# Root mean square of the SSD group by column quarters, and another order of output and pooling pieces

## The chip, the cores and the metric

The kernel runs on one core of a Trainium2 chip. The metric is the device time of one execution in microseconds (us), as the median of several executions. The engines are named as the profile names them: PE is TensorE (PEld its weight loads), DVE is VectorE, ACT is ScalarE, POOL is GpSimd and SP is SyncE, which here only issues DMAs.

## The reference, cut to what matters

One layer of a diffusion backbone: a normalised and modulated input goes through one input projection; part of it feeds a bidirectional state space scan (SSD), part of it feeds a pooling mixer; both outputs share one output projection, and an MLP follows. The change is in the last lines of the mixer:

```python
def mixer_out(y_scan, xs, z, u, d_skip, ssm_norm_w, pool_w, pool_scale, w_out, grid):
    b, l = xs.shape[:2]
    y = y_scan + d_skip.astype(jnp.float32)[:, None] * xs
    y = y.reshape(b, l, SSM_GROUPS, -1) * jax.nn.silu(z).reshape(b, l, SSM_GROUPS, -1)
    y = rmsnorm(y, ssm_norm_w.reshape(SSM_GROUPS, -1)).reshape(b, l, D_SSM)
    pm = pool_mixer(u, pool_w, pool_scale, grid)
    return jnp.concatenate([y, pm], axis=-1) @ w_out.astype(jnp.float32)
```

There are 1024 tokens (two blocks b of 512) and 1024 SSD channels in two groups g of 512. So the norm of `y` is over four quarters (b, g), each of 4 tiles of 128 channels by 512 tokens. Pooling has four windows, each with 256 channels and a 256x256 matrix; the output projection multiplies 1024 normalised SSD channels and 1024 pooled channels.

## The kernel before, in words

Channels stand on the 128 partitions and tokens along the free axis. A dense product keeps float accuracy with three matmuls per 128x128 tile: operands are split into a rounded high part and a remainder, and `mm3` (L165) issues high x high (L172), high x low (L174) and low x high (L175). Weights come in pieces of 128 output channels, loaded by SP (`load_raw`, L115), split by ACT (`whi`) and DVE (`wlo`) in `split_raw` (L122). The pool `wp` has two buffers of each, so two split pieces exist at a time. The list `order` (L130 to L140) fixes the order of the pieces, `next_piece` (L157) takes the next and splits one ahead.

After the scan the list `units` (L134) sets the stage that the change touches. A unit "u" i is the input projection of the i-th pooling tile (`box_input`, L910), after which `box_diff` (L926) takes the box means of an earlier tile on DVE and writes them to DRAM (`d_d`). A unit "o" i is the SSD half of the output projection for output tile i: `out_ssm` (L972), 48 matmuls for both blocks, evicted by ACT into `sg` and written to `o_d`. A unit "p" i is a pooling matrix: `pool_mm` (L982) loads the differences (`dr`, L986), splits them (`dh` on ACT, `dl` on DVE), multiplies (tile `pw`, 24 matmuls, 12 for each block), and evicts into `pm_hi` (ACT, L994) and `pm_lo` (DVE, L995). After each "p", two rows of a modulation matrix are loaded (`wa`, L786) and summed on DVE (L81). The second half of the output projection, `out_pool` (L1084), needs all `pm` and adds to what `out_ssm` wrote (`mix`, read back at L1067).

`y_norm` (L875) is a generator, advanced between units by `step` (L1012). It loads the four quarters (`yt`, L881), then does for each quarter in turn: four squares on ACT (`y_sq`), one round of four matmuls with 32 columns of ones (L202, `SumSq.round`), each into a quarter of the partitions of one PSUM bank, one copy of these partial sums to SBUF (`sq<-ry`), one matmul with the full matrix `c512` that adds the 128 partial rows (L213), and a reciprocal square root on ACT and DVE (logarithm, exponential, square and a correction step in two DVE instructions, L217 to L221). These are float matmuls, and each shows as two instructions in the trace. Then it scales and splits the quarter (`yn_hi`, `yn_lo`, L901 to L903). The fourth quarter's factor is in `rs_r` of the pool `ypool`; `esY.close()` (L1014) gives that pool's space to the next `box_diff` tiles.

The instructions are not run in the order of the text. The framework plans the order of each engine's queue before the run: among the instructions that its own reckoning of durations says are ready, the one that stands first in the program goes first. `after` (L90) adds an order without a wait: the first square stands after the last weight split issued so far, the first sum after the last matmul issued so far. Once planned, each queue is worked off in order.

Of the kernel before, what the change touches and what calls it, by code (L numbers as in the profile page):

```python
# [8 lines left out]
F32 = mybir.dt.float32  # L9
# [6 lines left out]
P = 128  # L16
KT = 8
T = 1024
TB = 512
# [24 lines left out]
def hybrid_block(ctx, tc, A):  # L44
# [23 lines left out]
    def dense_ps(name):  # L68
        return psd.tile([P, TB], F32, tag="d", name=name)

    def pair_ps(name):
        return psm.tile([P, 2, TB], F32, tag="m", name=name)
# [4 lines left out]
    def stt(out, in0, s, in1, op0, op1):  # L77
        return ve.scalar_tensor_tensor(out=out, in0=in0, scalar=s, in1=in1, op0=op0, op1=op1)
# [8 lines left out]
    def act(out, in_, f, bias=0.0, scale=1.0):  # L87
        return ac.activation(out=out, in_=in_, func=f, bias=bias, scale=scale)  # L88

    def after(ins, prev):  # L90
        tc.add_manual_dep(
            ins.ins, prev.ins.name,
            mybir.DependencyInfo(mybir.DependencyClass.NoSync, mybir.DependencyReason.DATA),
            reason="order")
        return ins
# [36 lines left out]
    for m in range(8):  # L132
        order += [W[PX + m], W[PZ + m]]
    units = [("u", 0), ("u", 1), ("u", 2), ("u", 3), ("u", 4), ("o", 0), ("u", 5), ("o", 1), ("u", 6), ("o", 2),  # L134
             ("u", 7), ("o", 3), ("o", 4), ("o", 5), ("p", 0), ("o", 6), ("p", 1), ("o", 7), ("p", 2), ("p", 3)]
    for kind, i in units:
        order.append({"u": W[PU + i], "o": A["w_out"][0, i], "p": ("pool", i)}[kind])
    for m in (0, 1, 2, 3, 4, 5, 6, 7, 2, 3, 4, 5, 6, 7):
        order.append(A["w_out"][1, m])
    order += [A["w_mlp1"][m] for m in (0, 4, 1, 5, 2, 6)] * 2  # L140
# [16 lines left out]
    def next_piece(ahead=1):  # L157
        i = used[0]
        used[0] += 1
        fetch(i + 1 + ahead)  # L160
        return loaded[i]
# [19 lines left out]

    class SumSq:
        def __init__(self, n, nk, name, pool):
            self.pair = pair_ps(name)
# [21 lines left out]
        def rstd(self, comb, r=None):  # L208
            n = self.n
            part = self.tmp()  # L210
            act(part, self.ps[:, :n], AF.Copy)
            tot = self.pair[:, 1]
            pe.matmul(tot[:, :n], M[comb], part, start=True, stop=True)  # L213
            q = self.tmp()
            if r is None:
                r = self.pool.tile([P, self.pool.width], F32, tag="rs_r", name="rs_r", bufs=1)[:, :n]
            act(q, tot[:, :n], AF.Ln, bias=eps)  # L217
            self.exp = act(r, q, AF.Exp, scale=-0.5)
            act(q, r, AF.Square)
            stt(q, tot[:, :n], EPS, q, ALU.add, ALU.mult)  # L220
            stt(r, q, -3.0, r, ALU.add, ALU.mult)  # L221
            return r

    def modulated(src, r, G, sh, hi, lo, pool):
# [125 lines left out]
    def step(g, n=1):  # L350
        for _ in range(n):
            next(g, None)
# [503 lines left out]
    def y_tile(i, name, dt=F32):  # L856
        return yq.tile([P, 4, TB], dt, tag=f"y{i}", name=name)
# [17 lines left out]
    def y_norm():  # L875
        yt = []
        for i, (b, g) in enumerate(BG):
            if i == 1:
                yield
            yt.append(y_tile(i, "yt"))  # L880
            sy.dma_start(yt[i], yg_d[4 * g : 4 * g + 4, :, b * TB : (b + 1) * TB].rearrange("k p t -> p k t"))  # L881
        yield
        r_t = y_tile(8, "y_rs")
        rs = []
        for i in range(4):
            ssq = SumSq(TB, 4, "ry", yp_)
            sq_t = y_tile(4 + i, "y_sq")
            for k in range(4):
                sq = ssq.add(yt[i][:, k], later=True, sq=sq_t[:, k])
                if i == 0 and k == 0:  # L890
                    after(sq, last_split[0])
            rnd = ssq.round()
            if i == 0:
                after(rnd, last_mm[0])
            rs.append(ssq.rstd("c512", r_t[:, i] if i < 3 else None))
            yield
        for i, (b, g) in enumerate(BG):
            hi = y_tile((4, 6, 0, 2)[i], "yn_hi", F32R)
            lo = y_tile((5, 7, 1, 8)[i], "yn_lo", F32R)
            for k in range(4):  # L900
                stt(yt[i][:, k], yt[i][:, k], V("ssm_w", 4 * g + k, 1), rs[i], ALU.mult, ALU.mult)  # L901
                act(hi[:, k], yt[i][:, k], AF.Copy)
                tt(lo[:, k], yt[i][:, k], hi[:, k].bitcast(F32), ALU.subtract)  # L903
            yn[b, g] = (hi, lo)
            yield
# [20 lines left out]
    def box_diff(gi, m, cu):  # L926
        wd = WINDOWS[gi]
        h2 = wd // 2
        lev = wd.bit_length() - 1
        nh = 1 if wd == 2 else 2  # L930
        ru_t = up.tile([P, (GR + WM - 1) * GW], F32, tag="ru", name="ru")
        ru = ru_t[:, : (GR + wd - 1) * GW].rearrange("p (a b) -> p a b", b=GW)
        gp.memset(ru[:, 0:h2, :], 0.0)
        if h2 > 1:
            gp.memset(ru[:, h2 + GR :, :], 0.0)
        nr = GR // nh
        for hf in range(nh):
            src, n = cu[:, hf * nr : (hf + 1) * nr, :], GW + wd - 1
            for l in range(lev):
                s_ = 1 << l  # L940
                n -= s_
                if l == lev - 1:
                    dst = ru[:, h2 + hf * nr : h2 + (hf + 1) * nr, :]
                else:
                    dst = box_tile("bc", l)[:, : nr * n].rearrange("p (a b) -> p a b", b=n)
                tt(dst, src[:, :, 0:n], src[:, :, s_ : s_ + n], ALU.add)
                src = dst
        for a, b in ((0, h2), (GW - h2 + 1, GW)):
            if a < b:
                sub = ru[:, h2 : h2 + GR, a:b]  # L950
                tt(sub, sub, edge[:, gi, GR + a : GR + b].unsqueeze(1).broadcast_to([P, GR, b - a]), ALU.mult)
        dv = up.tile([P, GR, GW], F32, tag="dv", name="dv")
        ncl = GW // nh
        for hf in range(nh):
            cs_ = slice(hf * ncl, (hf + 1) * ncl)
            src, n = ru[:, :, cs_], GR + wd - 1
            for l in range(lev):
                s_ = 1 << l
                n -= s_
                if l == lev - 1:  # L960
                    dst = dv[:, :, cs_]
                else:
                    dst = box_tile("br", l)[:, : n * ncl].rearrange("p (a b) -> p a b", b=ncl)
                tt(dst, src[:, 0:n, :], src[:, s_ : s_ + n, :], ALU.add)
                src = dst
        for a, b in ((0, h2), (GR - h2 + 1, GR)):
            if a < b:
                tt(dv[:, a:b], dv[:, a:b], edge[:, gi, a:b].unsqueeze(2).broadcast_to([P, b - a, GW]), ALU.mult)
        stt(dv, dv, 1.0 / (wd * wd), cu[:, :, h2 : h2 + GW], ALU.mult, ALU.subtract)
        sy.dma_start(d_d[m], dv.rearrange("p a b -> p (a b)"))  # L970

    def out_ssm(m):  # L972
        w = next_piece()
        for b in range(NB):
            ps = dense_ps("mixp")
            mm3(ps, w, yn[b, 0], kn=4, stop=False)
            mm3(ps, w, yn[b, 1], k0=4, kn=4, start=False)
            t = sg.tile([P, TB], F32, tag="sg", name="sg")
            act(t, ps, AF.Copy)
            sy.dma_start(o_d[b][:, m], t)  # L980
# [23 lines left out]
    for kind, i in units:  # L1004
        if kind == "u":
            gi = i // 2
            box.append((gi, i, box_input(gi, next_piece())))
            nu += 1
            if nu > 1:
                box_diff(*box.pop(0))  # L1010
            if nu in (2, 3, 4):
                step(yn_steps, (0, 0, 5, 2, 3)[nu])  # L1012
            if nu == 3:
                esY.close()  # L1014
                ux = new_pool(esU, "ux", 1)
        elif kind == "o":
            out_ssm(i)
            if box and nu == 8:
                box_diff(*box.pop(0))
        else:  # L1020
            if pm is None:
                esK.close()
                esU.close()
                pm = [(poolA.tile([P, KT, TB], F32R, tag="A", name=f"pm_hi{b}"),
                       poolA.tile([P, KT, TB], F32R, tag="A", name=f"pm_lo{b}")) for b in range(NB)]
                esD = ctx.enter_context(ExitStack())
                dp = new_pool(esD, "dp", 2, side="right")
                crow2 = dp.tile([P, 1024], F32, name="crow2", bufs=1)
                sy.dma_start(crow2, c_d.broadcast_to([P, 1024]))
            pool_mm(i)  # L1030
            for j in range(16 + 2 * i, 18 + 2 * i):
                ada_rest(j, dp.tile([P, 1024], F32, tag="wa2", name="wa2"), crow2)
# [594 lines left out]
```

## Time and profile before

| | |
|---|---|
| median of 3 runs | 1444.07 us (1443.58 to 1445.48) |
| profiled execution | 1443.95 us, its span 1442.2 us |
| PE busy | 1397.7 us, 97% of the span |
| DVE busy | 1034.1 us, 72% |
| ACT busy | 733.7 us, 51% |
| mean granted TensorE clock | 0.991 |
| `y_norm` sums on PE | 472.0 to 496.6 us |
| first `out_ssm` matmul on PE | 518.8 us |
| first and last `pw` matmul on PE | 617.1 and 669.1 us |

A stretch row gives the start and end in us, then the busy time of each engine with the number of instructions, then the granted clock (1.00 is the full 2.4 GHz), DMA share and GB/s. A timeline row gives start, busy time, engine, line, operation, output and inputs, shape and count, and in brackets the idle time before it with what ended it. An x2 in a row of L202 or L213 is one matmul in float. Matmuls are pipelined, so what one costs is read from the start of one to the start of the next.

### The profile page before, as it was taken

The numbers are of one execution on the slowest core, as the hardware profiler recorded it, in microseconds if no ns is written. First come the engines' busy times: TensorE is split into PE (matmuls) and PEld (weight loads), VectorE is DVE, ScalarE is ACT, GpSimd is POOL, SyncE is SP. The second block draws the span as 40 slices with busy tenths as digits, with TensorE's granted clock in tenths as the row PEclk, the third lists the DMA queues.
The fourth block names the chain that finished last, engine by engine and source line by source line (L and its number), as shares of the span: only waits on it lengthen the run. The fifth ranks groups of instructions, "written<-read, shape, count | busy, mean of one in ns | idle before, by whom it ended". The sixth has DMA issues, their size and how long they took to land. (4 is left out here: it accounts for less than half of the span.)

```text
span 1442.2 us, 18171 instructions
## 1 busy us (share of the span) xinstructions
PE 1397.7 (97%) x6760; PEld 1092.0 (76%) x6760; DVE 1034.1 (72%) x1606; ACT 733.7 (51%) x1150; POOL 49.3 (3%) x100
## 2 busy tenths in 40 slices
PE   6999899999999999999999999999999999999996
PEld 2667778888887588877866687888887888888875
DVE  2699589987776699663667776665668787878626
ACT  4776565555553732243246665555566562535344
POOL 0000100000000000000000000000001000000000
PEclk8999999999999999999999999999999999999998
DMA  9421644542223332479533444433467463645703
GB/s 386 163 66 55 135 135 136 151 108 78 79 75 97 134 103 102 147 258 379 193 117 110 139 170 173 158 135 134 149 215 258 143 209 96 186 136 168 249 21 117
DMA packets 77177, 218.60 MB, mean 152 GB/s; under 512 B 8993, under 2 KB 15265, under 8 KB 74658
## 3 DMA queue, kind: packets, MB, share of 16 engines
q1 hardware_dynamic: 67058, 186.25, 39.9%
q0 software_dynamic: 10032, 31.20, 5.9%
q8 instruction: 53, 0.87, 0.2%
q14 instruction: 34, 0.28, 0.1%
HBM read 164.07 MB, written 53.35 MB: 151 GB/s over the span
## 5 line engine op out<-in xcount | busy, mean ns | idle before, releaser
L172 PE MATMUL dn<-h_hi,whi 128*128 128x512 f32 x448 | 179.3, 400 | 1.1 <-ACT Cf L88 1.1
L174 PE MATMUL dn<-h_lo,whi 128*128 128x512 f32 x448 | 177.4, 396 | 0.0
L175 PE MATMUL dn<-h_hi,wlo 128*128 128x512 f32 x448 | 177.3, 397 | 0.0
L1242 PE MATMUL sx<-hop,wop 128*128 128x512 f32 x432 | 169.6, 392 | 1.4 <-ACT acc L88 1.4
L1243 PE MATMUL sx<-hop,wop 128*128 128x512 f32 x432 | 170.3, 394 | 0.0
L1244 PE MATMUL sx<-hop,wop 128*128 128x512 f32 x432 | 168.7, 391 | 0.0
L88 ACT ACTIVATE wop<-raw 128x512 fp32r<-128x512 f32 x162 | 101.1, 626 | 104.5 <-PE syw L1244 47.4
L85 DVE TENSOR_TENSOR wop<-raw,wop 128x512 fp32r<-128x512 f32 x162 | 111.4, 689 | 48.2 <-ACT wop L88 47.7
L88 ACT ACTIVATE whi<-raw 128x1024 fp32r<-128x1024 f32 (+1 forms) x76 | 78.6, 1034 | 129.5 <-PE mixp L174 52.1
L1242 PE MATMUL syw<-hop,wop 128*128 128x512 f32 x324 | 127.6, 394 | 2.8 <-DVE stage L85 2.8
L85 DVE TENSOR_TENSOR wlo<-raw,whi 128x1024 fp32r<-128x1024 f32 (+1 forms) x76 | 90.6, 1193 | 52.8 <-ACT whi L88 52.3
L1243 PE MATMUL syw<-hop,wop 128*128 128x512 f32 x324 | 128.1, 395 | 0.0
L1244 PE MATMUL syw<-hop,wop 128*128 128x512 f32 x324 | 127.0, 392 | 0.0
L172 PEld LDWEIGHTS dn<-h_hi,whi 128*128 128x128 f32 x448 | 84.2, 188 | 24.7 <-issue 7.4
L174 PEld LDWEIGHTS dn<-h_lo,whi 128*128 128x128 f32 x448 | 84.2, 188 | 22.1 <-issue 6.0
L175 PEld LDWEIGHTS dn<-h_hi,wlo 128*128 128x128 f32 x448 | 84.2, 188 | 20.4 <-issue 3.8
L88 ACT ACTIVATE hop<-hraw 128x512 fp32r<-128x512 f32 x116 | 70.9, 627 | 52.9 <-DMA hraw<-hid_d 52.3
L1242 PEld LDWEIGHTS sx<-hop,wop 128*128 128x128 f32 x432 | 81.2, 188 | 20.7 <-ACT acc L88 1.8
L1244 PEld LDWEIGHTS sx<-hop,wop 128*128 128x128 f32 x432 | 81.2, 188 | 18.2
L1243 PEld LDWEIGHTS sx<-hop,wop 128*128 128x128 f32 x432 | 81.2, 188 | 17.8
L85 DVE TENSOR_TENSOR hop<-hraw,hop 128x512 fp32r<-128x512 f32 x116 | 77.0, 687 | 13.0 <-ACT hop L88 12.7
L1242 PEld LDWEIGHTS syw<-hop,wop 128*128 128x128 f32 x324 | 60.9, 188 | 17.7 <-DVE stage L85 3.2
(315 smaller groups left out, 2838.0 us busy)
## 6 DMA issues: line engine op xcount, KB each, us to landing
raw<-in_w_mlp SPq DMA_DIRECT2D x70, 512.0 KB, 4.0
hraw<-hid_d SPq DMA_DIRECT2D x116, 256.0 KB, 3.2
raw<-in_w_in SPq DMA_DIRECT2D x38, 512.0 KB, 3.7
hid_d<-stage POOLq DMA_DIRECT2D x9, 1792.0 KB, 7.7
wa<-in_w_ada SPq DMA_DIRECT2D x24, 512.0 KB, 4.5
raw<-in_w_out SPq DMA_DIRECT2D x22, 512.0 KB, 3.9
wada<-in_w_ada SPq DMA_DIRECT2D x8, 1024.0 KB, 10.8
E<-rows_d SPq DMA_DIRECT2D x32, 256.0 KB, 4.4
```

The source lines that it names most:

```text
L85: eng.tensor_tensor(out=out, in0=a, in1=b, op=op)
L88: return ac.activation(out=out, in_=in_, func=f, bias=bias, scale=scale)
L172: ins = pe.matmul(out, a, r, start=start and k == 0, stop=False)
L174: pe.matmul(out, a, s, start=False, stop=False)
L175: last_mm[0] = pe.matmul(out, b, r, start=False, stop=stop and k == kn - 1)
L1242: pe.matmul(ps, a, r, start=start and k == 0, stop=False, skip_group_check=not start)
L1243: pe.matmul(ps, a, s, start=False, stop=False, skip_group_check=not start)
L1244: pe.matmul(ps, b_, r, start=False, stop=k == 3, skip_group_check=not start)
```

## The change

The four quarters are squared in one double loop with the tile k outside and the quarter i inside. All 16 sums go to one PSUM bank, quarter i into column group i (partitions 32i to 32i+31), accumulated over k. One copy takes the four sums to SBUF, and four matmuls with 32 rows of `c512` each write the totals of the four quarters to four PSUM banks. The reciprocal square roots of all four follow, by the function `newton`, which holds the instructions that were in `rstd`. The number of `step` calls is fitted. In `units`, the pooling matrices stand one by one between output pieces, and the last output piece is done in two halves, block 0 before the last pooling matrix and block 1 after it, with its split weights kept.

```diff
     units = [("u", 0), ("u", 1), ("u", 2), ("u", 3), ("u", 4), ("o", 0), ("u", 5), ("o", 1), ("u", 6), ("o", 2),
-             ("u", 7), ("o", 3), ("o", 4), ("o", 5), ("p", 0), ("o", 6), ("p", 1), ("o", 7), ("p", 2), ("p", 3)]
+             ("u", 7), ("o", 3), ("o", 4), ("p", 0), ("o", 5), ("p", 1), ("o", 6), ("p", 2), ("o", 7), ("p", 3),
+             ("h", 7)]
...
+    def newton(tot, pool, r=None):
+        n = tot.shape[-1]
+        q = pool.tile([P, pool.width], F32, tag="sq", name="sq", bufs=pool.nsq)[:, :n]
+        if r is None:
+            r = pool.tile([P, pool.width], F32, tag="rs_r", name="rs_r", bufs=1)[:, :n]
+        act(q, tot, AF.Ln, bias=eps)
+        ins = act(r, q, AF.Exp, scale=-0.5)
+        act(q, r, AF.Square)
+        stt(q, tot, EPS, q, ALU.add, ALU.mult)
+        stt(r, q, -3.0, r, ALU.add, ALU.mult)
+        return r, ins
...
         r_t = y_tile(8, "y_rs")
+        sq_t = [y_tile(4 + i, "y_sq") for i in range(4)]
+        for k in range(4):
+            for i in range(4):
+                ins = act(sq_t[i][:, k], yt[i][:, k], AF.Square)
+                if i == 0 and k == 0:
+                    after(ins, last_split[0])
+        ps = dense_ps("ry")
+        for k in range(4):
+            for i in range(4):
+                ins = pe.matmul(ps[32 * i : 32 * i + 32], M["ones"][:, :32], sq_t[i][:, k], start=k == 0, stop=k == 3)
+                if i == 0 and k == 0:
+                    after(ins, last_mm[0])
+        part = yp_.tile([P, TB], F32, tag="sq", name="sq", bufs=yp_.nsq)
+        act(part, ps, AF.Copy)
+        pairs = [pair_ps("ry") for _ in range(2)]
         rs = []
         for i in range(4):
-            ssq = SumSq(TB, 4, "ry", yp_)
-            sq_t = y_tile(4 + i, "y_sq")
-            for k in range(4):
-                sq = ssq.add(yt[i][:, k], later=True, sq=sq_t[:, k])
-                if i == 0 and k == 0:
-                    after(sq, last_split[0])
-            rnd = ssq.round()
-            if i == 0:
-                after(rnd, last_mm[0])
-            rs.append(ssq.rstd("c512", r_t[:, i] if i < 3 else None))
-            yield
+            pe.matmul(pairs[i // 2][:, i % 2], M["c512"][32 * i : 32 * i + 32], part[32 * i : 32 * i + 32],
+                      start=True, stop=True)
+        for i in range(4):
+            rs.append(newton(pairs[i // 2][:, i % 2], yp_, r_t[:, i] if i < 3 else None)[0])
+        yield
...
-    def out_ssm(m):
-        w = next_piece()
-        for b in range(NB):
+    kept = {}
+
+    def out_ssm(m, blocks=(0, 1)):
+        w = kept[m] if m in kept else next_piece()
+        kept[m] = w
+        for b in blocks:
...
-                step(yn_steps, (0, 0, 5, 2, 3)[nu])
+                step(yn_steps, (0, 0, 2, 2, 3)[nu])
...
-            out_ssm(i)
+            out_ssm(i, (0,) if i == 7 else (0, 1))
...
+        elif kind == "h":
+            out_ssm(i, (1,))
```

## Rows read from the trace of the kernel before

**Rows 1.** Busy time by stretch: all instructions, 500 to 600 and 617 to 670 us.

```profile
500.00:600.00 100.00, 99.92 (x441) 82.42 (x440) 93.97 (x136) 27.23 (x41) 4.13 (x16) 1.00 0.28 93
617.00:670.00 53.00, 49.99 (x214) 39.42 (x213) 31.29 (x45) 23.49 (x33) 0.00 (x0) 1.00 0.84 298
```

**Rows 2.** The same view, dense pieces (dn) alone, then the sums (ry).

```profile
471.91:496.57 24.66, 12.41 (x38) 6.44 (x38) 0.59 (x1) 1.00 0.41 154
...
471.91:496.57 24.66, 15.28 (x40) 3.24 (x40) 2.07 (x3) 4.46 (x8) 1.00 0.41 154
```

**Rows 3.** PE in order of time, around the sums.

```profile
471.68 0.39 PE L175 MATMUL dn<-h_hi,wlo 128*128 128x512 f32 x1
472.00 1.52 PE L202 MATMUL ry<-y_sq,mats 128*32 128x512 f32 x4
...
475.19 0.40 PE L175 MATMUL dn<-h_hi,wlo 128*128 128x512 f32 x1
475.51 1.04 PE L202 MATMUL ry<-y_sq,mats 128*32 128x512 f32 x2
...
476.83 0.40 PE L174 MATMUL dn<-h_lo,whi 128*128 128x512 f32 x1
...
477.52 1.02 PE L213 MATMUL ry<-sq,mats 128*128 128x512 f32 x2
478.47 1.38 PE L202 MATMUL ry<-y_sq,mats 128*32 128x512 f32 x6
...
493.46 1.05 PE L202 MATMUL ry<-y_sq,mats 128*32 128x512 f32 x2
...
496.58 0.40 PE L174 MATMUL dn<-h_lo,whi 128*128 128x512 f32 x1
```

**Rows 4.** PE in order of time, one later round of sums, four matmuls together.

```profile
726.41 0.39 PE L175 MATMUL mixp<-pm_hi,wlo 128*128 128x512 f32 x1
726.73 1.06 PE L202 MATMUL mms<-sq,mats 128*32 128x512 f32 x8
...
728.06 0.39 PE L174 MATMUL mixp<-pm_lo,whi 128*128 128x512 f32 x1
```

**Rows 5.** PE in order of time, three matmuls of 18 rows in the scan.

```profile
382.47 0.50 PE L743 MATMUL arg<-RH,LH 18*128 18x512 f32 x3
```

**Rows 6.** PE in order of time, end of the scan, the matmuls of one PSUM tile.

```profile
456.59 0.43 PE L771 MATMUL y<-D,xst 128*64 128x128 f32 x2
456.96 0.49 PE L172 MATMUL dn<-h_hi,whi 128*128 128x512 f32 x1
457.38 1.09 PE L771 MATMUL y<-D,xst 128*64 128x128 f32 x14
```

**Rows 7.** ACT in order of time, first quarter's squares and the copy after them.

```profile
471.28 2.18 ACT L88 ACTIVATE y_sq<-yt 128x512 f32<-128x512 f32 x4
476.60 0.60 ACT L88 ACTIVATE sq<-ry 128x512 f32<-128x512 f32 x1 [3.14 <-PE ry L202]
```

**Rows 8.** The tile yt: its four loads (start of first and last), and issue to landing.

```profile
L881 SPq DMA_DIRECT2D yt<-yg_d x4: 360/372/514, 462.5 to 466.1; - x4
...
DMA to landing us min/median/max: 6.8/11.8/13.1
```

**Rows 9.** DVE in order of time: first and last of the box differences, a modulation sum.

```profile
514.46 0.70 DVE L85 TENSOR_TENSOR bc<-cu 128x528 f32<-128x528 f32 x1
...
600.62 1.23 DVE L78 SCALAR_TENSOR_TENSOR dv<-dv,cu 128x1024 f32<-128x1024 f32 x1
...
635.77 1.23 DVE L81 SCALAR_TENSOR_TENSOR wa<-wa,crow 128x1024 f32<-128x1024 f32 x1 [5.65 <-DMA wa<-in_w_ada]
```

**Rows 10.** All engines in order of time, the first pooling matrix.

```profile
610.45 1.06 ACT L88 ACTIVATE dh<-dr 128x1024 fp32r<-128x1024 f32 x1 [3.12 <-DMA dr<-d_d]
...
617.12 0.40 PE L172 MATMUL pw<-dh,whi 128*128 128x512 f32 x1
```

**Rows 11.** PE in order of time, second pooling matrix.

```profile
638.86 0.50 PE L172 MATMUL pw<-dh,whi 128*128 128x512 f32 x1 [1.75 <-DVE pm_lo L78]
```

More of the change, by code (lines that the diff above doesn't have):

```diff
@@ L134, in hybrid_block @@
     units = [("u", 0), ("u", 1), ("u", 2), ("u", 3), ("u", 4), ("o", 0), ("u", 5), ("o", 1), ("u", 6), ("o", 2),
-             ("u", 7), ("o", 3), ("o", 4), ("o", 5), ("p", 0), ("o", 6), ("p", 1), ("o", 7), ("p", 2), ("p", 3)]
+             ("u", 7), ("o", 3), ("o", 4), ("p", 0), ("o", 5), ("p", 1), ("o", 6), ("p", 2), ("o", 7), ("p", 3),
+             ("h", 7)]
     for kind, i in units:
-        order.append({"u": W[PU + i], "o": A["w_out"][0, i], "p": ("pool", i)}[kind])
+        if kind != "h":
+            order.append({"u": W[PU + i], "o": A["w_out"][0, i], "p": ("pool", i)}[kind])
     for m in (0, 1, 2, 3, 4, 5, 6, 7, 2, 3, 4, 5, 6, 7):
@@ L213, in rstd @@
             pe.matmul(tot[:, :n], M[comb], part, start=True, stop=True)
[L214 to L221, printed above, removed]
+            r, self.exp = newton(tot[:, :n], self.pool, r)
             return r
```

## The prediction

> **What bounds the kernel now.** I looked first at the busy time by stretch. From 500 to 600 us PE is busy 99.92 of 100 us at the full clock of 2.4 GHz, with 441 matmuls, so one dense matmul takes 100/441 = 0.227 us of PE's time; DVE is nearly as full, 93.97 us [rows 1]. In the pooling stage, 617 to 670 us, PE idles 3.0 of 53 us, at the same clock [rows 1]. So PE is the bound, and an edit counts by the PE time that it saves or loses, unless it makes PE wait. Next I read how much of PE the norm's sums take. From 471.91 us (the start of the last dense matmul before them plus 0.227) to 496.57 us PE issues 38 dense matmuls and 40 instructions of the sums [rows 2, 3]. The dense ones are worth 38 x 0.227 = 8.6 us, so the sums cost 24.7 - 8.6 = 16.0 us of PE.
>
> Then I read why, in PE's order of time. The four matmuls with `c512` stand 0.95 us apart from what follows (477.52 to 478.47), 3.8 us in all [rows 3]. That leaves 12.2 us for 16 sums. They stand in ten blocks between dense matmuls, the first of two sums at 472.00, the last of one at 493.46: blocks of 2, 1, 1, then 3, 1, and the same again [rows 3]. A block of one takes 475.19 to 476.83 less two dense matmuls, 1.19 us. A block of four, in a later norm, takes 726.41 to 728.06 less two dense matmuls, 1.20 us [rows 4]. Four sums side by side in four column groups cost PE the same as one. What counts is the number of blocks, and 12.2/10 = 1.2 us each agrees.
>
> **The sums after the change.** The number of squares and sums stays 16; the number of blocks may change, and the planner's order decides that. Two rows tell how it plans. First, it keeps the matmuls of one PSUM tile in program order: one goes out, then a dense matmul while the second waits for its input, then the other seven, although the third had its input when the first had [rows 6]. So the new sums keep the order k outside, quarter inside. Second, it reckons that the second quarter comes late: ACT is idle 3.14 us before the first copy, and a square of the second quarter, had the planner thought it loaded, would stand in that gap [rows 7]. The trace gives it reason: the loads start from 462.5 to 466.1 us, a first lands after 6.8 us, the last after 13.1 us, at 479.2 us [rows 8]. So ACT will square the four tiles of each quarter as it lands, and on PE the sum of quarter 0 goes alone, that of quarter 1 alone, that of quarter 2 alone; the first sum of quarter 3 frees a run: it and three sums of the next k together, twice more the same, and one at the end. Seven blocks: 7 x 1.2 = 8.4 us. Ends: four blocks, 4.8 us; sixteen blocks, 19.2 us. I take 8.4, as it follows from the two rows.
>
> **The totals.** Four matmuls of 32 rows take the place of four full ones. No row shows this shape. The nearest is three matmuls of 18 rows in three row groups, which together last 0.50 us, where three dense ones one after the other take 0.68 [rows 5]; so row groups run side by side. Below: one block as above, 1.2 us. Above: one after the other, 3.8 us. I take 1.2, nearest to that row. By TensorE: Matmul & The Clock Gate in the Trainium skill, section on packing small matmuls, four row tiles reach 3.07 times the rate, which makes 3.8/3.07 = 1.24 us, an estimate, and the sum would be the same within 0.1.
>
> A rule on the same page, in the same part, speaks against the change: weight loads overlap running matmuls only where the row group differs, and column groups share all rows. By it a block of four would cost four times one. The row of four sums in 1.20 us disagrees, so I give it no weight.
>
> So the norm costs PE 8.4 + 1.2 = 9.6 us in place of 16.0: **6.4 us less**. Three copies on ACT (0.60 us each) go; ACT is not the bound [rows 1, 7].
>
> **Waits that the norm can add.** ACT works its queue in order, so a square of quarter 3 that is planned too early holds the evictions of dense pieces behind it, and PE waits for its sum until 479.2 + 0.6. PE can be there at the earliest after three blocks, 472.0 + 3.6 = 475.6 us: 0 to 4.2 us of wait. I take 0.5, because the planner reckons the loads late and puts dense matmuls between. The sums now hold one of the three dense PSUM buffers until the copy; with two left, an eviction has 24 x 0.227 = 5.4 us, the next block's length, and takes about 0.6: nothing.
>
> All four reciprocal roots come at the end: 12 ACT and 8 DVE instructions in a row instead of between rounds. Scaling starts later but runs unbroken. DVE's box differences begin at 514.46, once the last scaling has freed the pool `ypool` [rows 9]. I take that point as unmoved; a shift to 512 or 517 is possible either way. The first output piece needs only the first two quarters: nothing.
>
> **The new order of units.** Each pooling matrix brings along on SP one weight load, two `dr` and two `wa` loads, two splits on ACT and two on DVE, four evictions on each and two modulation sums on DVE; all of it is moved ahead of one output piece (its weight load, split and two stores), the last by half a piece. POOL has nothing in either. What has a price:
>
> - The first matrix can't start before the last box difference is done (600.62 + 1.23 us) and its loads have landed and been split: `dh` starts at 610.45, so first matmuls from 611.5 us. Before, PE got there at 617.12 [rows 9, 10]. With PE 5.9 us ahead it is there at 611.2, since the piece that stands behind it in the list fills in. That is a wait of 0.3 us, 0 to 6 if DVE ends later. I take 0.5.
> - PE's 3.0 us of idle time in the stage [rows 1]: the largest, 1.75 us, ends on `pm_lo` [rows 11], and there DVE had stood 5.65 us for a `wa` load [rows 9]; the rest is at the last two matrices, which stand together before and get half a piece between them now. Gain 0 to 3.0, loss 0 to 3 where a DVE that waits for `wa` hits the new place. I take 1.0 gained.
> - The kept weights of output piece 7 hold a buffer to the end, so the weights of the first `out_pool` piece are split only when the last matrix is through, 1.06 + 1.22 us; the half piece behind it covers that (24 x 0.227 = 5.4 us). The reads of `mix` come later too, behind the last half piece; PE has two free PSUM buffers, 10.9 us, before it needs them. Nothing; if the cover is gone, some 2 us.
>
> **Sum**: -6.4 + 0.5 + 0.5 - 1.0 = -6.4 us against the profiled execution's 1443.95 us (span 1442.2 and 1.75 around it), which is 0.1 below the median: 1437.6 us. About 0.2% (2.9 us) is what a measurement of this kernel can tell from no change.
>
> **Rivals.**
> - *The gain is held up at pooling.* DVE is full to 600 us [rows 1]. If the later roots push its box differences back by some 5 us, the first matrix starts about where it did, PE having only one piece to fill with (the two weight buffers are taken). For: DVE's 87 us from 514.46 to 601.85 have little idle time. Against: scaling runs unbroken. About 1442.5 us, no difference. Chance 0.18.
> - *Slower: the sums stand singly.* If the planner reckons the four loads together and early, squares come one by one, quarter by quarter, and PE fills every gap with dense matmuls, as it did within each round. Sixteen blocks: 16 x 1.2 + 1.2 = 20.4 against 16.0, 4.4 slower, 1447.8 us with the order of units worth half. It decides from (16.0 - 1.2)/1.2 = 12.4 blocks on. For: ten blocks for 16 sums now. Against: rows 6 and 7. The page TensorEngine Tiling (Array Packing) of the Trainium skill, under Key Properties, says that a change of tiling mode drains the engine; the 1.19 us of a lone block is consistent with it. Chance 0.15.
> - *Better.* The run after quarter 3 is unbroken (13 sums, 3.4 us, instead of four blocks) and pooling loses its idle time: 1.4 and 2 us more, and no waits: 1433 us. Chance 0.12.
> - *The totals don't run side by side* and the change doesn't do what it says there: 2.6 us back, 1440.2 us. Chance 0.03.
>
> **How the numbers follow.** The forecast has 0.52. Faster by over 0.2%: 0.52 + 0.12 + 0.03 = 0.67; within: 0.18; slower: 0.15. The forecast's own range from its bounds is 1434 to 1441; to leave out no more than 2 in 10 the range takes in the held-up case and most of the slower and the better one: 1432 to 1446.
>
> **What would show it.** Right: `ry` on PE in about seven blocks, the longest after 479 us; the `c512` matmuls as one block near 1.2 us; first `out_ssm` matmul near 513 instead of 518.8; first `pw` near 612 or before; PE's idle time in pooling under 3 us. Wrong: `ry` in more than 12 blocks; idle PE before a sum with ACT named; idle PE of several us before the first `pw` with DVE or a `dr` load named.

## The result and the profile after

The changed kernel is slower: 1454.84 us median of 7 runs (1450.46 to 1458.9) against 1445.28 of 7 runs of the kernel before (1442.09 to 1446.39), ratio 1.0067 with a 95% interval of 1.005 to 1.0085, some 9.6 us. The forecast was 1437.6 (1432 to 1446).

| | before | after |
|---|---|---|
| median, us | 1445.28 | 1454.84 |
| profiled execution, its span | 1443.95, 1442.2 | 1458.09, 1456.3 |
| PE busy | 1397.7 (97%) | 1400.3 (96%) |
| DVE busy | 1034.1 (72%) | 1033.6 (71%) |
| ACT busy | 733.7 (51%) | 731.9 (50%) |
| mean granted clock | 0.991 | 0.986 |

The profiled execution is one of the longer ones, and part of its 14.1 us has nothing to do with the change: 1.7 us stand there before the norm begins (the scan has the same instructions in both), and 3.6 us come behind the output projection, 2.6 of them where PE waits 5.42 us for DVE's `stage` in place of 2.81; with the instructions there unchanged, that wait took from 2.83 (e10) to 5.39 us (e8) in other kernels of this study. So I read the change from two stretches of the profiles. **Norm stage**: from the weight split on DVE just before the norm (`wlo`, 470.93 us before, 472.65 after) to the last `dn` matmul of the pooling inputs (584.25, 588.32): 113.32 us became 115.67, **+2.35**. **Output stage**: from there to the last `mixp` matmul (766.27, 776.79): 182.02 became 188.47, **+6.45**. The sum, 8.8, is about the difference of the medians.

PE in order of time around the sums, after:

```profile
473.68 1.05 PE L900 MATMUL ry<-y_sq,mats 128*32 128x512 f32 x2 [1.92 <-ACT y_sq L88]
...
476.92 1.04 PE L900 MATMUL ry<-y_sq,mats 128*32 128x512 f32 x2
...
481.30 1.05 PE L900 MATMUL ry<-y_sq,mats 128*32 128x512 f32 x2
...
485.68 3.62 PE L900 MATMUL ry<-y_sq,mats 128*32 128x512 f32 x26
...
490.36 1.14 PE L908 MATMUL ry<-sq,mats 32*128 32x512 f32 x8
491.43 0.50 PE L177 MATMUL dn<-h_hi,wlo 128*128 128x512 f32 x1
```

This part came as forecast, against [rows 3]: three lone sums, then all the rest from the first sum of the fourth quarter on, 13 sums in one run (L900, x26, two instructions each), and the four totals as one block of 1.07 us up to the next start. From 471.60 to 491.43 us 41 dense matmuls start, so the sums and totals cost 19.83 - 41 x 0.227 = 10.5 us, 1.92 of it idle. The forecast was 9.6 and a wait of 0.5. Counted the same way, by their starts, the dense matmuls of the kernel before are 37 and not 38 (the view also counts one that was still running at 471.91), so its sums cost 16.3 us and not 16.0. At 491.43 us the change is 5.8 us ahead, and then it loses 8.1 us.

The idle 1.92 us stand ahead of the first sum in all five kernels of this study that keep the 16 sums in one dense buffer (the changed one, e1, e3, e4 and e7) and in no other: there the planner put the first sum nine dense matmuls earlier than before, and PE waits for the first square.

Busy time by stretch, after (columns as in [rows 1]):

```profile
500.00:600.00 100.00, 95.69 (x406) 77.59 (x405) 93.72 (x137) 27.89 (x44) 4.11 (x16) 0.97 0.26 90
617.00:670.00 53.00, 52.47 (x229) 42.38 (x228) 34.29 (x48) 25.20 (x35) 0.00 (x0) 1.00 0.65 217
500.00:520.00 20.00, 16.90 (x61) 12.96 (x60) 19.31 (x31) 12.24 (x21) 0.00 (x0) 0.83 0.09 27
```

From 500 to 600 us PE issues 406 matmuls in place of 441 [rows 1], and the clock is down to 0.83 from 500 to 520. From 617 to 670 us the idle time went from 3.0 to 0.5 us. That window flatters the new order: it leaves out two waits that the order brings just ahead of the first matrix.

```profile
611.39 0.50 PE L174 MATMUL mixp<-yn_hi,whi 128*128 128x512 f32 x1 [0.92 <-ACT whi L88]
...
615.19 0.50 PE L174 MATMUL pw<-dh,whi 128*128 128x512 f32 x1 [0.43 <-ACT dh L88]
```

With them the idle time around the matrices is 1.9 us against 3.0.

PE in order of time shows where the 500s lose:

```profile
504.71 0.39 PE L176 MATMUL dn<-h_lo,whi 128*128 128x512 f32 x1
507.77 0.79 PE L174 MATMUL mixp<-yn_hi,whi 128*128 128x512 f32 x1 [2.67 <-ACT cu L88]
508.36 0.63 PE L176 MATMUL mixp<-yn_lo,whi 128*128 128x512 f32 x1
509.42 0.80 PE L177 MATMUL dn<-h_hi,wlo 128*128 128x512 f32 x1 [0.44 <-DVE wlo L85]
...
514.29 0.56 PE L176 MATMUL dn<-h_lo,whi 128*128 128x512 f32 x1
514.68 0.39 PE L177 MATMUL dn<-h_hi,wlo 128*128 128x512 f32 x1
```

PE idles until an eviction of ACT (`cu`) frees a PSUM buffer and until DVE has the low part of a weight piece (`wlo`). After that stop 14 matmuls take 6.9 us, to 514.68: most of them 0.43 us apart, the 1.2 GHz level, where 0.227 is usual. What stood ahead of those two on their engines, in order of time: first the start of scaling on DVE before, then DVE after, then ACT after:

```profile
484.35 2.74 DVE L78 SCALAR_TENSOR_TENSOR yt<-yt,vec,y_rs 128x512 f32<-128x512 f32 x4
```

```profile
493.58 0.69 DVE L78 SCALAR_TENSOR_TENSOR sq<-ry,sq 128x512 f32<-128x512 f32 x1 [7.99 <-ACT sq L88]
494.30 0.69 DVE L78 SCALAR_TENSOR_TENSOR y_rs<-sq,y_rs 128x512 f32<-128x512 f32 x1
495.03 2.74 DVE L78 SCALAR_TENSOR_TENSOR yt<-yt,vec,y_rs 128x512 f32<-128x512 f32 x4
...
508.15 1.22 DVE L85 TENSOR_TENSOR wlo<-raw,whi 128x1024 fp32r<-128x1024 f32 x1
...
518.97 0.70 DVE L85 TENSOR_TENSOR bc<-cu 128x528 f32<-128x528 f32 x1
```

```profile
504.47 1.29 ACT L88 ACTIVATE yn_hi<-yt 128x512 fp32r<-128x512 f32 x2 [1.21 <-DVE yt L78]
505.67 1.04 ACT L88 ACTIVATE whi<-raw 128x1024 fp32r<-128x1024 f32 x1
506.62 0.61 ACT L88 ACTIVATE yn_hi<-yt 128x512 fp32r<-128x512 f32 x1
507.14 0.58 ACT L88 ACTIVATE cu<-dn 128x512 f32<-128x512 f32 x1
```

DVE stands idle for 8 us until the first total has come (at 490.36), starts scaling at 495.03 (484.35 before), and the scaling is 2.8 us later at the box differences (518.97 less 514.46 [rows 9], less the 1.7 of the start). The eviction at 507.14 stands behind a `yn_hi` that waits for DVE's scaling.

The second loss is at the start of the output projection's second half. The two reads of `xr` (the layer's input for the residual, 2 MB each) before and after; then, for the weight loads (`raw`) issued from 660 to 700 us, issue to landing before and after; the weight split on ACT and the matmul behind it, after; and the stretch from 675 to 700 us with the DMA share (next to last column), before and after:

```profile
L1071 SPq DMA_DIRECT2D xr<-in_xT x2: 333/360/386, 649.7 to 653.8; - x2
```

```profile
L1092 SPq DMA_DIRECT2D xr<-in_xT x2: 333/390/447, 674.7 to 675.4; - x2
```

```profile
DMA to landing us min/median/max: 3.7/6.8/10.6
```

```profile
DMA to landing us min/median/max: 3.6/17.6/17.6
```

```profile
699.58 1.06 ACT L88 ACTIVATE whi<-raw 128x1024 fp32r<-128x1024 f32 x1 [2.24 <-DMA raw<-in_w_out]
```

```profile
700.69 0.50 PE L174 MATMUL mixp<-pm_hi,whi 128*128 128x512 f32 x1 [2.25 <-ACT whi L88]
```

```profile
675.00:700.00 25.00, 25.00 (x112) 20.70 (x111) 12.42 (x17) 5.92 (x7) 0.00 (x0) 1.00 0.69 250
```

```profile
675.00:700.00 25.00, 22.98 (x99) 17.31 (x97) 6.33 (x9) 3.33 (x5) 0.00 (x0) 1.00 1.02 404
```

`xr` is issued 25 us later than before, right behind the eight reads of `mix` (666.34 to 674.74), and some 8 MB are issued in ten microseconds. The weight loads issued next, at 681.88 and 684.42, land after 17.6 us, and PE waits for them. From 695.80 us (the last dense matmul before the stop plus 0.227) to 705.94 PE starts only 12 dense matmuls, worth 2.7 us: it idles 2.25 us for `whi`, 0.46 and 0.53 for two other inputs, and then runs at the lower clock (granted clock 0.83 from 700 to 710). Four sums of the next norm (`mms`), one block before (703.74 us), stand in three blocks here.

### The profile page after: what moved, and what is told of

Its sections match the earlier page's. It is cut to its first block, busy times and chain, and to the rows that moved or that the text cites. A ratio compares the mean times of both kernels' runs of the same rounds, so it can differ in the third digit from the quotient of the medians.

```text
span 1456.3 us, 18157 instructions
## 1 busy us (share of the span) xinstructions
PE 1400.3 (96%) x6760; PEld 1095.5 (75%) x6760; DVE 1033.6 (71%) x1606; ACT 731.9 (50%) x1147; POOL 49.3 (3%) x100
## 5 line engine op out<-in xcount | busy, mean ns | idle before, releaser
L88 ACT ACTIVATE whi<-raw 128x1024 fp32r<-128x1024 f32 x76 | 78.5, 1033 | 132.2 <-PE mixp L176 51.0
L85 DVE TENSOR_TENSOR wlo<-raw,whi 128x1024 fp32r<-128x1024 f32 x76 | 90.6, 1194 | 48.6 <-ACT whi L88 48.1
```

What stands on the lines that cost most here:

```text
L85: eng.tensor_tensor(out=out, in0=a, in1=b, op=op)
```

## The experiments

Two losses were to be explained. Theory A said of the first that the four roots in a row delay scaling, and with it DVE's and ACT's queues, and of the second that the order of units with its half pieces makes the reads late. The times stand in the table below, each with its own runs of the kernel before; norm and output are the two stretches as shifts against the profile of before, in us; the last column is how much later than there the first scaling starts, counted from the start of the norm stage.

| kernel | median (before) | ratio, 95% interval | norm | output | scaling |
|---|---|---|---|---|---|
| changed | 1454.84 (1445.28) | 1.0067, 1.005 to 1.0085 | +2.35 | +6.45 | +9.0 |
| e1 norm only | 1449.17 (1446.7) | 1.0024, 1.0007 to 1.004 | +3.21 | -0.22 | +10.6 |
| e2 order only | 1452.02 (1446.7) | 1.0037, 1.0024 to 1.005 | +0.04 | +8.12 | 0.0 |
| e3 xr late | 1446.56 (1446.7) | 1.0006, 0.9988 to 1.0024 | +2.27 | -0.74 | +9.0 |
| e4 roots spread | 1458.91 (1446.7) | 1.0082, 1.0059 to 1.0104 | +3.70 | +6.57 | +10.5 |
| e5 sums in pair buffer | 1447.03 (1445.31) | 1.0007, 0.9987 to 1.0028 | +3.20 | -0.53 | +9.0 |
| e6 two groups | 1442.96 (1445.31) | 0.9977, 0.996 to 0.9993 | -3.32 | -0.87 | +2.0 |
| e7 wlo first | 1446.04 (1445.31) | 0.9994, 0.9973 to 1.0014 | +1.78 | 0.00 | +10.6 |
| e8 old norm, order, xr late | 1446.71 (1445.31) | 1.0005, 0.9983 to 1.0028 | +0.01 | -0.12 | 0.0 |
| e9 last square first | 1434.94 (1446.21) | 0.9929, 0.991 to 0.9947 | -8.26 | -0.88 | -3.3 |
| e10 two groups, old order | 1443.33 (1446.21) | 0.9986, 0.997 to 1.0002 | -3.37 | -0.64 | +2.0 |
| e11 last square, order, xr late | 1433.24 (1446.86) | 0.992, 0.9896 to 0.9945 | -8.25 | -0.19 | -3.3 |

**The two halves of the change alone.** e1 has the new norm and the old list of units (without the half pieces); its edit against the changed kernel is below. e2 has the old norm with the change's list of units, half pieces and kept weights.

```diff
-             ("u", 7), ("o", 3), ("o", 4), ("p", 0), ("o", 5), ("p", 1), ("o", 6), ("p", 2), ("o", 7), ("p", 3),
-             ("h", 7)]
+             ("u", 7), ("o", 3), ("o", 4), ("o", 5), ("p", 0), ("o", 6), ("p", 1), ("o", 7), ("p", 2), ("p", 3)]
...
-            out_ssm(i, (0,) if i == 7 else (0, 1))
+            out_ssm(i)
```

> The changed norm with the old order of units. Theory A (two losses: the norm stage loses about 2.4 us net, because all reciprocal roots come at the end and PE then waits behind ACT's evictions and runs part of the stage at 1.2 GHz; the order of units loses about 6 us at the read-back): 1446 to 1449 us, PE idle near 505 us as in the changed kernel, no idle time of PE near 698 us. Theory B (the norm gains its 5 to 6 us, and the order of units costs all of the loss): 1438 to 1440 us.

> The norm of before with the new order of units and the halved last output piece. Theory A: 1449 to 1453 us, xr read behind mix, weights for the output projection landing some 15 us after issue, PE idle near 690 us. Theory B: 1454 us or more. If the order of units is harmless by itself and only collides with an earlier PE: 1443 to 1446 us.

Each loss goes with its half: e1 loses in the norm stage and not in the output stage, e2 the other way round. In e2 the weight loads from 660 to 700 us land late and PE waits as in the changed kernel, though PE gets there no earlier than before:

```profile
DMA to landing us min/median/max: 3.5/18.4/18.4
```

```profile
698.77 0.79 PE L174 MATMUL mixp<-pm_hi,whi 128*128 128x512 f32 x1 [1.91 <-ACT whi L88]
```

**The reads of xr.** e3 is the changed kernel with the two reads of `xr` moved to output pieces 3 and 5 of the second half, each behind the last weight load issued by then.

```diff
-        sy.dma_start(raw[:, :k], src)
+        last_raw[0] = sy.dma_start(raw[:, :k], src)
...
-    for b in range(NB):
-        xr.append(poolB.tile([P, KT, TB], F32, tag="B", name="xr"))
-        sy.dma_start(xr[b], A["xT"][b])
...
+        if m in (3, 5):
+            xr.append(poolB.tile([P, KT, TB], F32, tag="B", name="xr"))
+            after(sy.dma_start(xr[-1], A["xT"][len(xr) - 1]), last_raw[0])
```

> The changed kernel, with the two xr reads (2 MB each) issued behind the weight loads of output pieces 3 and 5 of the second half instead of right behind the mix reads. Theory A (the 4 MB of xr, pushed back by the last half piece that still reads yn, delay the weights and modulation rows behind them): 6 to 8 us below the changed kernel, 1446 to 1449 us, no PE idle near 698 us. Rival (the kept weights of piece 7 hold the buffer and the weights of the second half come late for that): no difference from the changed kernel, 1452 to 1456 us.

```profile
L1164 SPq DMA_DIRECT2D xr<-in_xT x2: 382/382/383, 685.3 to 696.4; - x2
```

```profile
DMA to landing us min/median/max: 3.6/8.7/10.4
```

The output stage goes from +6.45 to -0.74, and the weight loads land in 10.4 us at most. The reads of `mix` and the split weights of piece 7, kept to the end, are as in the changed kernel, so neither is the cause: it is `xr` ahead of the weight loads. e8 (e2 with the same edit) shows it for the old norm: +8.12 becomes -0.12.

> The norm of before, the new order of units with the half pieces (as e2), and the xr reads behind the raw loads of the third and fifth... piece of the output projection's second half (as e3). Theory X (the reads of xr took the DMA time of the weight loads): the shift of +7.8 us in the output projection of e2 falls to 0.5 or less, no PE idle time over 1 us near 698; with the pooling stage 1 us better, the kernel stands at 0 to 2 us below the kernel before of the same job. If the order of units loses time in another way, 1447 us or more.

e8 also answers what the order of units is worth by itself: its time is that of the kernel before.

**The roots.** e4 is the changed kernel with the roots of the third and fourth quarter behind the scaling of the first and second.

```diff
-        for i in range(4):
+        def root(i):
             rs.append(newton(pairs[i // 2][:, i % 2], yp_, r_t[:, i] if i < 3 else None)[0])
+        root(0)
+        root(1)
...
+            if i < 2:
+                root(i + 2)
```

> The changed kernel, with the roots of quarters 2 and 3 placed behind the scaling of quarters 0 and 1 in the program; same instructions. Theory A (the four roots in a row make scaling late and put evictions behind waits for it): PE idle near 505 us and the stretch at 1.2 GHz go or shrink to under 2 us; 4 to 8 us below the changed kernel, 1446 to 1450 us. Rival (the sums hold one of three dense PSUM buffers): the wait near 505 us stays and the time is that of the changed kernel, 1452 to 1456 us.

Nothing was gained: the first scaling starts later still (+10.5), the norm stage is at +3.70, and the idle time before the first `mixp` matmul is 2.74 us on `cu`. Theory A's form of the first loss, the roots in a row, fell. Two were left. Theory B: it is the totals that are late, since all four wait for the fourth quarter; the roots can't start before 490 however they are ordered. Rival P: the sums' PSUM tile takes one of the three dense buffers, and PE's wait on `cu` is a wait for a buffer.

**PSUM or late totals.** e5 to e7 start from e3, so that the output stage is out of the way. e5 puts the sums in a pair buffer, e6 works in two groups of two quarters (the loops over `i` run over `j, j + 1`, with a copy, two totals and two roots for each group, sums in a pair buffer as e5), e7 adds an order on DVE and moves one step of the norm one unit later.

```diff
-        ps = dense_ps("ry")
+        ps = pair_ps("ry")[:, 0]
```

> The changed kernel with the xr reads late (as in e3), and the 16 sums in one of the two pair buffers of PSUM in place of one of the three dense buffers. Theory B (late DVE): the totals of all four quarters come in one block near 490 us, so DVE, idle until then, starts scaling some 10 us later than before and is full from there; the low parts of the weights (wlo) and, through yn_hi, the evictions on ACT stand behind the scaling, and PE waits near 508. By it this edit changes nothing: PE idle of 2 to 4 us between 504 and 513 stays, the clock falls below 0.95 in 500 to 520, and the norm stage (455 to 535 us, shift against the kernel before) stands at +1.5 to +3. Rival P (PSUM): the sums' tile leaves two dense buffers, and the wait that ends on the eviction cu is for a buffer; then the idle time is gone, the clock is 1.00, and the norm stage stands at -3 to -6.

```profile
519.76 0.66 PE L176 MATMUL dn<-h_hi,whi 128*128 128x512 f32 x1 [4.05 <-ACT cu L88]
...
524.36 0.79 PE L179 MATMUL mixp<-yn_hi,wlo 128*128 128x512 f32 x1 [3.51 <-DVE wlo L85]
```

The third dense buffer moved the stop by 10 us and made it longer, with the same two releasers; the wait before the first sum is gone, and the norm stage is at +3.20 all the same. Rival P fell.

```diff
+        for j in (0, 2):
...
-            for i in range(4):
+            for i in (j, j + 1):
```

> As e5, but the quarters in two groups of two: sums, one copy, two totals and the roots of quarters 0 and 1 first, then those of 2 and 3. Theory B: the first totals come near 479 us in place of 490, the first scaling near 484 to 487 (495 in the changed kernel, 484.35 in the kernel before), DVE has no idle time of 8 us before it, no PE idle time over 1 us between 495 and 515, clock 1.00 there; the sums cost some 8 blocks of 1.2 us with the totals, 9.6 us against 16.0, so the norm stage stands at -3 to -6 and the kernel at 1437 to 1442 us, 3 to 8 us below the kernel before of the same job. If the loss comes from the sums themselves or from PSUM in another way, PE idles near 508 as before and the time is that of e3, 1446 to 1448.

PE and DVE in order of time, e6, and its stretch from 495 to 530 us:

```profile
472.81 1.04 PE L905 MATMUL ry<-y_sq,mats 128*32 128x512 f32 x2
476.05 3.62 PE L905 MATMUL ry<-y_sq,mats 128*32 128x512 f32 x14
480.73 1.13 PE L913 MATMUL ry<-sq,mats 32*128 32x512 f32 x4
...
489.89 1.13 PE L913 MATMUL ry<-sq,mats 32*128 32x512 f32 x4
```

```profile
487.18 1.41 DVE L78 SCALAR_TENSOR_TENSOR yt<-yt,vec,y_rs 128x512 f32<-128x512 f32 x2
```

```profile
495.00:530.00 35.00, 34.89 (x154) 28.56 (x153) 34.55 (x56) 15.58 (x26) 1.03 (x6) 1.00 0.21 68
```

The first totals come some 9 us earlier, the first scaling 7 us earlier (+2.0 in place of +9.0), and PE has no stop from 495 to 530 (34.89 of 35 us busy, clock 1.00). The sums cost more than in the changed kernel: 24 dense matmuls from 472.72 to 490.95 leave 18.23 - 24 x 0.227 = 12.8 us, 3.5 less than before. Nearly all of that is kept, -3.32 in the norm stage, where the changed kernel's 5.8 turned into +2.35. Theory B holds.

```diff
-        tt(lo[:, :k], raw[:, :k], hi[:, :k].bitcast(F32), ALU.subtract)
+        last_lo[0] = tt(lo[:, :k], raw[:, :k], hi[:, :k].bitcast(F32), ALU.subtract)
...
+                if i == 1 and k == 0:
+                    after(ins, last_lo[0])
...
-                step(yn_steps, (0, 0, 2, 2, 3)[nu])
+                step(yn_steps, (0, 0, 2, 1, 4)[nu])
```

> As e3 (one group of four, sums in a dense buffer), with one order added on DVE: the first scaling of the second quarter stands behind the low part (wlo) of the weights of the fifth pooling input piece. Totals and roots are as late as in e3. Theory B: wlo runs near 504 in place of 508, PE's idle time between 504 and 513 (3.2 us and more) falls below 1.5 us, the clock stays over 0.97, and the norm stage stands at -1 to -4 against +2.3 in e3; the scaling ends as late as before or later. Rival P: the idle time that ends on the eviction cu stays at 2 us or more, since that waits for a dense buffer.

This missed: +1.78 in the norm stage, and PE idles later, for the next weight piece.

```profile
505.78 1.22 DVE L85 TENSOR_TENSOR wlo<-raw,whi 128x1024 fp32r<-128x1024 f32 x1
...
521.11 0.50 PE L177 MATMUL dn<-h_hi,whi 128*128 128x512 f32 x1 [2.42 <-ACT whi L88]
```

The low part named came first, and the stop near 508 shrank to 0.33 us, but the wait moved on to the piece behind it. The norm stage is 0.5 us better than in e3, from which e7 starts, and 1.4 better than in e1, whose first scaling was as late (+10.6); single profiles of the same norm differ by 0.9, so a gain is not shown. That the backlog as a whole loses the time, and not one instruction in a wrong place, fits this but is argued, not shown.

**A version that keeps both.** What made the sums dear was the number of blocks, and what made the changed kernel lose was that all totals waited for the last quarter. e9 keeps the kernel before, a round and a total for each quarter, and reverses the four sums of a round, so that none starts before the last square is there.

```diff
-        def round(self):
+        def round(self, order_=range(4)):
...
-                             start=self.k == 0, stop=self.k + 4 == self.nk) for g in range(4)]
+                             start=self.k == 0, stop=self.k + 4 == self.nk) for g in order_]
...
-            rnd = ssq.round()
+            rnd = ssq.round((3, 2, 1, 0))
```

> The kernel before, with one edit: in the SSD group's norm the four sums of a quarter stand in reverse order, the sum of the last square first, so that none starts before all four squares are there. The work is the same. If PE's cost of the sums is the number of blocks (step of the prediction: 1.2 us a block, whether it holds one sum or four), four blocks in place of ten save 6 x 1.2 = 7.2 us less what the wait for the last square adds; DVE's scaling starts within 1.5 us of the kernel before (484.35), so PE does not wait near 508 (theory B): norm stage at -5 to -7, the kernel 4 to 7 us below the kernel before. If blocks do not set the cost (each sum costs its share wherever it stands), or if fewer blocks lose as much by later scaling: 0 to -2 us.

```profile
474.59 1.07 PE L202 MATMUL ry<-y_sq,mats 128*32 128x512 f32 x8
475.59 0.50 PE L174 MATMUL dn<-h_lo,whi 128*128 128x512 f32 x1
...
476.62 1.02 PE L213 MATMUL ry<-sq,mats 128*128 128x512 f32 x2
...
478.27 1.06 PE L202 MATMUL ry<-y_sq,mats 128*32 128x512 f32 x8
```

```profile
482.01 1.41 DVE L78 SCALAR_TENSOR_TENSOR yt<-yt,vec,y_rs 128x512 f32<-128x512 f32 x2
...
511.15 0.70 DVE L85 TENSOR_TENSOR bc<-cu 128x528 f32<-128x528 f32 x1
```

Four blocks of four sums (x8) in place of ten. From 474.50 to 490.60 us 34 dense matmuls leave 16.10 - 34 x 0.227 = 8.4 us for sums and totals: 7.9 saved, and the norm stage shows -8.26. With fewer blocks in the way the totals come earlier, and scaling starts 3.3 us earlier than before. At 1434.94 us, 11.3 below the kernel before, e9 beats both kernels by more than was expected of it; the profile accounts for 9.7 of that.

The last two ask again for the order of units, with an earlier PE. e10 is e6 with e1's edit (and the reads of `xr` where they were), e11 is e8 with e9's edit.

> The two groups of e6 with the order of units of the kernel before and without the half pieces, so that the xr reads go out as early as there. If the order of units is worth nothing by itself (as e8 against the kernel before says, 1446.7 against 1445.3), the time is that of e6 within 1.5 us, 2 to 4 us below the kernel before, the norm stage at -3; if the order gives about 1 us in the pooling stage, e10 stands 1 us above e6.

> The norm of e9 (one round of four sums a quarter, the last square first) with the change's order of units and half pieces and the late xr reads (as e8). If the order of units is worth what the prediction's pooling term says (1.0 us gained, 0.5 lost at the first matrix), the pooling stage with PE about as early as in e9 gives 0.5 to 1 us more than e9: ratio to the kernel before 0.992 to 0.993, the shift from the end of the pooling inputs (about 580 us) to the end of the output projection (about 765 us) at -1 to -2 us. If the order is worth nothing, that shift is that of e9, -0.9 us, or above, and the ratio 0.993 or above.

e10 and e6 agree within a microsecond (ratios 0.9986 and 0.9977, their intervals overlap), and so do e11 and e9 (0.992 and 0.9929). The output stage of e11 is at -0.19, of e9 at -0.88. The new order of units is worth nothing that these runs can tell.

## Why the prediction was wrong

It forecast a gain and there was a loss of more than the range allowed for. By its steps:

- **Cost of a block, 1.2 us alike for one or four sums**: right. e9 changes nothing but the number of blocks, from ten to four, and saves 7.9 us of PE, where 6 x 1.2 is 7.2. That by the rule on weight loads a block of four would cost four times one was the prediction's own inference; four took 1.00 us in e9. Two of its figures are a little off and change nothing: two of the four totals before cost 0.86 us and not 0.95, and the slower rival's turning point is 12.3 blocks, not 12.4.
- **Sums 8.4, totals 1.2, a wait of 0.5**: nearly right in sum, 10.5 us for 10.1, with other parts, so part of the agreement is luck. The sums and totals cost 8.6, as the 13 sums ran unbroken (the better rival's first half), and the wait was 1.9: the announced sign, idle PE before a sum with ACT named, came, but before the first sum and not before the fourth quarter's. The saving was 16.3 - 10.5 = 5.8 us, where 5.9 was forecast.
- **"I take that point as unmoved; a shift to 512 or 517 is possible either way"** (the roots at the end): this is the first step that failed. The point moved by 2.8 us of its own (4.5 in all), just past its bound. But the step priced only the end of DVE's work. It left out what stands in the same queues in between: weight splits and evictions, for which PE waits. The delay was set by the totals, which all wait for the fourth quarter and come at 490 us; DVE was busy 9.27 of 13.67 us from 482.90 on before, and 5.61 of the same stretch after (from 484.62 on, 1.72 later as the start of the stage). That work was still to be done when PE needed `wlo` and `cu`. PE lost 2.83 us to 507.77 and 0.4, 1.0 and 0.3 us at three later stops, and the 14 matmuls at the lower clock cost 14 x 0.227 = 3.2 where they took some 6.5: together 7.8 of the 8.1 us lost.
- **"with two left, an eviction has 24 x 0.227 = 5.4 us ... nothing"** (PSUM): right as a cause, since a third buffer gains nothing in e5; wrong in its premise that an eviction takes about 0.6 us, as it can stand behind a `yn_hi` that waits.
- **Order of units, 0.5 lost and 1.0 gained**: the announced sign came (idle time in pooling 0.5 of 53 us in place of 3.0), but 1.35 us of other idle time had moved ahead of that window, and e8 against before, and e11 against e9, show no gain. The first `pw` matmul came at 615.19 us where near 612 was announced, as PE was late and not early.
- **"The reads of `mix` come later too ... Nothing; if the cover is gone, some 2 us"**: the second step that failed, and the larger loss. It followed the reads of `mix` alone. The two reads of `xr` stand behind them in SP's queue. Before, the first had gone out at 649.7 us, when its space, last read by `out_ssm`, came free; with the last half piece at the end of the stage the burst falls just ahead of the weight loads. The step should have counted every DMA that the move puts ahead of the loads that PE waits for, 8 MB here. Price: 6.45 to 8.1 us; with `xr` late, nothing.
- **The rivals**: the held-up one had the right first half, that later roots delay DVE, but put the price at pooling, and at no loss. The slower one, sums standing singly, did not happen. That a late DVE reaches PE through the weight splits and evictions at 504 us was in no case.

The page TensorE: Matmul & The Clock Gate of the Trainium skill, in the section on the array's architecture, says that the queues of ScalarE and VectorE are strictly first in, first out. The trace agrees: the eviction `cu` at 507.14 us runs behind a `yn_hi` that waited 1.21 us for DVE's scaling. The prediction used this for the squares and not for the scaling.

Not settled is why the same new norm costs +2.3 in two profiles and +3.2 in e1; the first scaling is 1.6 us later there. And it was not tried whether some full order of ACT's and DVE's queues would keep the gain with totals as late as these.

## What to carry to other kernels

When sums are merged so that a later group comes in one go, ask not only what PE saves but when the first result now comes, and what else the waiting engines have in their queues: work that bunches up behind one late total delays weight splits and evictions which have nothing to do with it. When a step is moved, follow the transfers behind it on the queue to the next load that the bound engine needs. And where a planner sends out whatever is ready, letting the group's last input be read first turns many small blocks into one, at no cost in work.

## What the runs showed of the hardware

- Four float matmuls of 32 rows in four row groups cost PE 1.07 us up to the next start (490.36 to 491.43), two of them 1.06 (e6), where one with 128 rows between sums costs 0.95 [rows 3]. By the Trainium skill, TensorE: Matmul & The Clock Gate, section on packing small matmuls, four row tiles run 3.07 times as fast. Here, with float matmuls, it is 4 x 0.95/1.07 = 3.6 from start to start. Counted to the second dense matmul behind, less one dense, a total costs 0.86 (482.91 to 484.00 before) and the four 1.17 (490.36 to 491.76), and it is 2.9; so the trace agrees as well as it can tell.
- Four sums in four column groups took 1.00 us to the next start (474.59 to 475.59 in e9), one sum alone 0.97 to 0.98 (the two-instruction blocks of e8, and 473.88 to 474.85 before).
- After the stop of 2.83 us, matmuls ran at the 1.2 GHz level for 6.9 us (granted clock 0.83 from 500 to 520 us), which cost 3.3 us, more than the stop itself. In e5, with stops of 4.05 and 3.51 us, the granted clock was 0.50 from 520 to 530.
- A weight load of 0.5 MB issued at 665.92 us, after 4 us without DMA traffic, landed in 3.6 us; issued behind some 8 MB it landed in 17.6 us, while 404 GB/s went through.
